# Two down projections of a macaron layer: block sums by accumulating transfers, operands and sums made at earlier steps, and a mixer planned from a running clock

## The chip, the cores and the metric

One Trainium2 chip, one of its cores. The metric is device time in microseconds of one launch, as the median over runs; the profile is one execution of the same program, read by the time from the first to the last of its own instructions (the span). All inputs and outputs are float32.

## The reference

One decoder layer on x of 512 tokens by 1024 channels; the middle mixer is only named here.

```python
D_MODEL, SEQ, D_FF = 1024, 512, 2816

def rmsnorm(x, g):
    return x * lax.rsqrt(jnp.mean(x * x, axis=-1, keepdims=True) + EPS) * g

def swiglu(x, w_gate, w_up, w_down):
    return (jax.nn.silu(x @ w_gate) * (x @ w_up)) @ w_down

x = x + 0.5 * swiglu(rmsnorm(x, ffn1_norm), ffn1_wg, ffn1_wu, ffn1_wd)
x = x + hybrid_mixer(rmsnorm(x, mix_norm), ...)   # sparse attention and a gated recurrence
x = x + 0.5 * swiglu(rmsnorm(x, ffn2_norm), ffn2_wg, ffn2_wu, ffn2_wd)
out = rmsnorm(x, final_norm)
```

## The kernel before, in words

**Precision.** TensorE multiplies in its rounded float32 form. To keep the precision of float32, each operand is split into a rounded part and a remainder: ScalarE (ACT) copies with rounding (`wh`, `yh`, the lower half of a `cm` tile), VectorE (DVE) subtracts that from the source (`wl`, `yl`, the upper half). A product is three matmuls: part by part, part by remainder, remainder by part. So whatever TensorE (PE) is to multiply passes ACT and then DVE first.

**Stages.** Up projection of the first feed-forward block, its down projection `d1`, the mixer, up projection and down projection `d2` of the second block, final norm. Both down projections are written by `block_down` (line 596); its steps are emitted one after the other, in the order in which every engine runs them (the schedule is manual; each engine runs its own instructions in the order of the program).

**A down projection.** D_FF is 22 tiles of 128 rows. Six tiles (`PLAIN`) are multiplied plainly, in steps `("D", half, k)`. The other sixteen form eight pairs (`PAIRS`), and for these a product of 2 by 2 blocks is made of seven products in place of eight (Strassen's scheme in Winograd's form), on sums and differences of blocks. Products are numbered 1, 2, 5, 6, 3, 7, 4 in the order in which they run, eight steps `(p, j)` each, one for each pair. So the steps are (line 604): six plain steps 0 to 5; products 1, 2 and 5 at 6 to 29; product 6 and then product 3, each of eight steps with two plain steps of the second half between them (30 to 39, 40 to 49); product 7 (50 to 57), two plain steps (58, 59), product 4 (60 to 67). In `d1` a step of a product is twelve matmuls of 256 columns, in `d2` six of 512; a plain step is twelve of 512.

**What a step needs.** Two things, both made some steps ahead by `task(i, f)`, which runs `f` behind step `i`:

- *A unit of weights*, split at step i - 4 (`unit`, `wsplit`). For products 1, 4 and 2 it is a block as loaded (`raws`, three buffers of 512 KB, loaded by SyncE's queue, SP). For the others it is a sum of blocks of the weights. Product 5's is block 2 + block 3: `base` loads block 2 with SP into `sums[j]`, `add` adds block 3 with an accumulating transfer that GpSimd (POOL) issues. Product 6's adds block 0 to it: `one` loads it with SP into a work tile (`a1`, four buffers), `second` adds it on DVE. Product 3's adds block 1 to that: `two` loads it with SP into another work tile (`a2`, three buffers), `fourth` adds it on DVE (lines 719 to 727). Product 7's is a sum of its own, block 2 + block 0, in a tile `s3[j]`: a load by SP at i - 15 and an add by POOL at i - 13.
- *An operand* made of the activations, split by `operand(p, j, soon)` `before` steps ahead (line 729): 9 for product 4, 5 for product 3. For product 4 the remainder is not made by DVE: ACT writes the negated rounded part, and POOL adds the source by an accumulating transfer within SBUF. Its source is written by a DVE subtraction one step earlier into the half `b(j)[:, hi]`, the half that product 3 reads.

`sums[j]` lies in two large tiles, four sums each, in `d1` (shown as `sm` in the profile) and in the tiles of x in `d2` (shown as `x`); `s3` tiles and operands (`cm`) are taken from a pool of 60 slots of 128 by 512 floats, which also holds the blocks of activations (`h`). DVE also adds each finished product to the residual (`x` in `d1`, `xr` in `d2`: `results1`, `results`), which must be done before PE may go on in the same bank: product 4 goes on in the banks that product 7 used.

**The end of `d1`.** While product 7 and product 4 run, the first four channel tiles of the mixer's operand are made (`norm_tile`, line 946, one each at steps 51, 53, 55 and 57), the others in two halves (`norm_round`), and their squares are summed into `acc`.

**The mixer.** Its 64 weight jobs run in an order written out by hand (`ORDER`, line 49): one job is one column tile of a projection. Everything else (norm, sparse attention, recurrence, gates) is a set of generators that `tick` (line 1183) advances between PE's matmuls as soon as a planner (`Plan`, line 60) says that their inputs will be there. The planner keeps a clock for each engine and a ready time for each tile, from fixed costs of each instruction. `plan.clear()` empties it behind `d1`, and `run_jobs` (line 1209) calls `plan.rewind()`, which sets all clocks to zero and forgets all ready times, and then gives `acc` a ready time of 2.6 us. The first five jobs (`i0 i1 k0 v0 e0`) use the unscaled operand `y`; the following ones use the normalised one, which exists once `acc` is complete, PE has summed and turned it, and eight tiles have been scaled and split.

All instructions are recorded under line 173 (the planner's `call`) and all transfers under line 161, so the profile is read by the tiles' names.

Of the kernel before, what the change touches and what calls it, by code (L numbers as in the profile page):

```python
# [12 lines left out]
ALU = mybir.AluOpType  # L13
# [33 lines left out]


ORDER = """
i0 i1 k0 v0 e0 q0 x0 x1 q1 x2 r1 x3 g0 q2 x4 g1 g2 q3 x5 g3 r2 x6  # L50
g4 r3 g5 x7 a0 r4 g6 a1 r5 g7 r6 a2 a3 a4 a5 r7 a6 a7 R0 R1 R2 R3
R4 R5 R6 A0 A1 A2 A3 A4 A5 A6 R7 A7 O0 O1 O2 O3 O4 O5 O6 O7
"""

V_G1, V_GM, V_G2, V_GF = 0, 8, 16, 24
# [4 lines left out]
class Plan:  # L60
# [8 lines left out]
    def clear(self):  # L69
        self.time = dict.fromkeys(("PE", "DVE", "ACT", "POOL", "SP", "DMA"), 0.0)  # L70
        self.ready, self.read, self.writer, self.table = {}, {}, {}, None
        self.live = {}

    def rewind(self):
        self.time = dict.fromkeys(self.time, 0.0)
        self.ready, self.read, self.writer = {}, {}, {}

    def seen(self, name, by):

# [99 lines left out]
def hybrid_kernel(ctx, tc, xt, vec, w1u, w1d, wm, wki, wrg, watt, wrnn, wout, w2u, w2d, gf, out):  # L179
    nc = tc.nc  # L180
    plan = Plan()
    V, A = plan.engine("DVE", nc.vector), plan.engine("ACT", nc.scalar)
    G, T = plan.engine("POOL", nc.gpsimd), plan.engine("PE", nc.tensor)
    Q = plan.engine("SP", nc.sync)
# [26 lines left out]
    def awork(name="a"):  # L211
        return patt.tile([P, S], F32, tag="att", name=nm(name))
# [383 lines left out]
    def block_down(hs, wd, sums):  # L596

        d = Down()
        steps = [("D", 0, k) for k in range(PLAIN)] + [(p, j) for p in (1, 2, 5) for j in range(PAIRS)]
        for p in (6, 3):
            for j in range(PAIRS):
                steps += [(p, j)] + [("D", 1, (6, 3).index(p) * 2 + j // 3)] * (j in (2, 5))
        steps += [(7, j) for j in range(PAIRS)] + [("D", 1, k) for k in (4, 5)] + [(4, j) for j in range(PAIRS)]
        index = {s: i for i, s in enumerate(steps)}
        tasks = {}  # L610

        def task(i, *fs):
            tasks.setdefault(i, []).extend(fs)

        def block(b, j):

            i, half = b * (PAIRS // 2) + j // 2, j % 2 * S
            return wd[i][:, half:half + S]

        units, turned, ra, raws, s3, ones, twos = {}, {}, {}, {}, {}, {}, {}  # L620

        def fetch(key, i):
            def load():
                raws[key] = raw.tile([P, WMAX], F32, tag="raw", name=nm("wr"))
                Q.dma_start(raws[key], wd[i])

            return load

        def unit(i, src):
            def split_():  # L630
                if i % 2 == 0:
                    units[i // 2] = [wsp.tile([P, WMAX], F32R, tag=t, name=nm(t)) for t in ("wh", "wl")]
                wsplit(src(), *(t[:, i % 2 * S:(i % 2 + 1) * S] for t in units[i // 2]))

            return split_

        a = lambda j: hs[PLAIN + 2 * j]
        b = lambda j: hs[PLAIN + 2 * j + 1]

        def differences(j):  # L640
            def subs():
                if j % 2 == 0:
                    ra[j // 2] = slot(F32, "cr")
                V.tensor_sub(ra[j // 2][:, (lo, hi)[j % 2]], a(j)[:, hi], b(j)[:, hi])
                V.tensor_sub(a(j)[:, hi], a(j)[:, hi], a(j)[:, lo])

            return subs

        SRC = {1: lambda j: a(j)[:, lo], 5: lambda j: a(j)[:, hi], 6: lambda j: a(j)[:, lo], 3: lambda j: b(j)[:, hi],
               7: lambda j: ra[j // 2][:, (lo, hi)[j % 2]], 4: lambda j: b(j)[:, hi], 2: lambda j: b(j)[:, lo]}  # L650

        def operand(p, j, soon):
            def make():
                o, src = slot(F32R, "cm"), SRC[p](j)
                turned[p, j] = o
                sign = -1.0 if p in (1, 3) else 1.0
                A.activation(o[:, lo], src, AF.Copy, scale=sign)
                if sign < 0:
                    V.scalar_tensor_tensor(o[:, hi], src, -1.0, f(o[:, lo]), op0=ALU.mult, op1=ALU.subtract)
                elif soon:  # L660
                    V.tensor_sub(o[:, hi], src, f(o[:, lo]))
                else:
                    A.activation(o[:, hi], src, AF.Copy, scale=-1.0)
                    G.dma_start(o[:, hi], src, accum_op=ALU.add)

            return make

        used = []
        for i, st in enumerate(steps):
            if st[0] == "D":  # L670
                _, h, k = st
                key = ("D", h, k // 2)
                if k % 2 == 0:
                    used.append([i - 4, index["D", h, k + 1] - 4, key, 2 * PAIRS + h * (PLAIN // 2) + k // 2])
                task(i - 4, unit(i, lambda key=key, k=k: raws[key][:, k % 2 * S:(k % 2 + 1) * S]))
                continue
            p, j = st
            if p in (1, 4, 2):
                key = (p, j // 2)
                if j % 2 == 0:  # L680
                    used.append([i - 4, index[p, j + 1] - 4, key, {1: 0, 2: 1, 4: 3}[p] * (PAIRS // 2) + j // 2])
                src = lambda key=key, j=j: raws[key][:, j % 2 * S:(j % 2 + 1) * S]
            elif p == 7:
                src = lambda j=j: s3[j]
            else:
                src = lambda j=j: sums[j]
            if p == 1:
                task(j, differences(j))
            if p == 5:
                def base(j=j):  # L690
                    Q.dma_start(sums[j], block(2, j))

                def add(j=j):
                    G.dma_start(sums[j], block(3, j), accum_op=ALU.add)

                task(j + 2, base)
                task(j + 4, add)
            if p == 7:
                def base(j=j):
                    s3[j] = slot(F32, "s3")  # L700
                    Q.dma_start(s3[j], block(2, j))

                def add(j=j):
                    G.dma_start(s3[j], block(0, j), accum_op=ALU.add)

                task(i - 15, base)
                task(i - 13, add)
            if p == 6:
                def one(j=j):
                    ones[j] = work("a1")  # L710
                    Q.dma_start(ones[j], block(0, j))

                def second(j=j):
                    V.tensor_add(sums[j], sums[j], ones[j])

                task(i - 9, one)
                task(i - 5, second)
            if p == 3:
                def two(j=j):
                    twos[j] = awork("a2")  # L720
                    Q.dma_start(twos[j], block(1, j))

                def fourth(j=j):
                    V.tensor_add(sums[j], sums[j], twos[j])

                task(i - 8, two)
                task(i - 5, fourth)
            soon = p != 4
            before = {1: 6, 6: 6, 7: i - j - 1, 4: 9}.get(p, 5)
            if p == 6:  # L730
                task(i - before - 1, lambda j=j: V.tensor_sub(a(j)[:, lo], b(j)[:, hi], a(j)[:, hi]))
            if p == 4:
                task(i - before - 1, lambda j=j: V.tensor_sub(b(j)[:, hi], b(j)[:, lo], a(j)[:, lo]))
            task(i - before, operand(p, j, soon))
            task(i - 4, unit(i, src))
        used.sort()
        for n, (first, last, key, i) in enumerate(used):
            at = first - 5
            if n >= RAWS:
                at = max(at, used[n - RAWS][1])  # L740
# [47 lines left out]
    y = []  # L788
# [14 lines left out]
    sums = []  # L803
# [139 lines left out]
    then1 = lambda i, f_, *a: late1.setdefault(i, []).append((f_, a))  # L943

    for k in range(KD // 2):
        then1(index[7, 0] + 1 + 2 * k, lambda k=k: y.append(norm_tile(k, V_GM)))
    rounds = {k: norm_round(k, hi) for k in range(KD // 2, KD)}
    for k in range(KD // 2, KD):
        then1(index[4, k - KD // 2], next, rounds[k], None)
# [4 lines left out]
    then1(index[4, 4], mixer_prepare)  # L954
    with tc.manual_schedule(engines=ENGINES):
        assert min(d1.tasks) >= 0
        cs = decay()
        for i in range(last):
            if i == 0:
# [42 lines left out]

    plan.clear()
    for h, l in y:
        plan.take("slot", h), plan.take("slot", l)
    follow = []
# [200 lines left out]
    def run_jobs():  # L1209
        ws = mixer_ws  # L1210
        mixer_fetch()
        mixer_fetch()
        plan.rewind()
        plan.ready[acc.name], plan.writer[acc.name] = 2.6, "DVE"
        for i, job in enumerate(jobs):
            ys, then = uses[job[0]](int(job[1:]))
            n, m = columns(job)
# [567 lines left out]
```

## Time and profile before

| what | us |
|---|---|
| median of 3 runs | 1084.09 |
| lowest and highest | 1083.97, 1086.08 |
| the profiled execution, in all | 1082.94 |
| its span | 1081.1 |
| PE, DVE, ACT, POOL busy | 1066.5, 863.3, 662.4, 139.9 |
| first down projection | 235 to 353 of the span |
| mixer | 353 to 730 |
| second down projection | 955 to 1074 |

How to read it. Times in the profile's rows are microseconds from the start of the span, unless they are marked ns. In a timeline a row is: start, duration, engine, line, operation, what it writes `<-` what it reads, shape, count, and in brackets the idle time of that engine before it and what ended it. A row of the chain is: start, length, engine and tile. A row of transfers is: tile `<-` source, issuing queue, operation, count, KB each, median us from issue to landing. A row of a window is: from:to, its length, then for PE, weight loads, DVE, ACT and POOL the busy time and the number of instructions, PE's granted clock, the mean busy share of the 16 DMA engines and GB/s. A matmul's recorded length is longer than the time until the next can start, so waits of PE are best read from start to start.

### The profile page before, as it was taken

To read this page: it belongs to the slowest core of one execution; us is meant where nothing else is said; L and a number is where in the kernel's file an instruction comes from. 1 tells how busy PE (TensorE), PEld (TensorE's weight loads), DVE (VectorE), ACT (ScalarE), POOL (GpSimd) and SP (SyncE) were. 2 spreads that over 40 slices of the span, in tenths; PEclk is the share of its full clock that TensorE was granted. 3 is DMA by queue.
4 is the path that set the end of the run, shared out by engine and by line. 5 is a ranking of instruction groups with operands and counts; after the bars stand their busy time and mean duration, and the time that the engine had idled before them with its cause. 6 is when DMAs were issued, how large, how long until landed. Compare 5 with 4: busy or idle time off the path is not lost.

```text
span 1081.1 us, 17665 instructions
## 1 busy us (share of the span) xinstructions
PE 1066.5 (99%) x6412; PEld 945.3 (87%) x6412; DVE 863.3 (80%) x1668; ACT 662.4 (61%) x1313; POOL 139.9 (13%) x171
## 2 busy tenths in 40 slices
PE   9999999999999999999999999999999999999997
PEld 7889999999988778888888888888899999987776
DVE  6687777779988879999799867666877777777887
ACT  6565655555547659868885664345656555565555
POOL 0161111102023000000000000002511111101022
PEclk9999999999999999999999999999999999999999
DMA  7297777739487452232232213435977777459395
GB/s 274 69 253 195 171 181 196 174 111 266 132 220 173 136 143 89 83 103 78 79 98 80 77 38 83 133 98 131 244 173 194 161 193 192 110 150 269 117 247 152
DMA packets 74007, 163.90 MB, mean 152 GB/s; under 512 B 8768, under 2 KB 17088, under 8 KB 73920
## 3 DMA queue, kind: packets, MB, share of 16 engines
q1 hardware_dynamic: 51216, 128.11, 36.6%
q0 software_dynamic: 22272, 34.09, 20.1%
q8 instruction: 50, 0.82, 0.3%
q10 hardware_dynamic: 432, 0.57, 0.1%
q14 instruction: 37, 0.30, 0.1%
HBM read 151.73 MB, written 2.10 MB: 142 GB/s over the span
## 4 chain that ended last, share of the span: by engine, by line
PE 85%; DVE 8%; ACT 2%; DMA 2%; issue 2%; SPq 0%; ACTq 0%; DVEq 0%
PE mm L173 59%; PE aux L173 27%; DVE wl L173 2%; ACT wh L173 1%; DMA wr<-w2d 1%; DVE x L173 1%; DVE sm L173 1%; DMA s<-w1d 1%; DVE yl L173 1%; DVE cm L173 1%; DMA x<-xt 0%; DVE acc L173 0%; DVE yf L173 0%; ACT yh L173 0%; DVE h L173 0%
## 5 line engine op out<-in xcount | busy, mean ns | idle before, releaser
L173 PE MATMUL mm<-cm,wh 128*128 128x256 f32 x1472 | 268.8, 283 | 1.6 <-DVE x L173 1.6
L173 DVE TENSOR_TENSOR wl<-wr,wh 128x512 fp32r<-128x512 f32 (+2 forms) x228 | 189.1, 833 | 78.1 <-ACT wh L173 77.8
L173 PEld LDWEIGHTS mm<-cm,wh 128*128 128x128 f32 x1472 | 229.9, 192 | 2.8 <-ACT cm L173 2.0
L173 PE MATMUL mm<-cm,wl 128*128 128x256 f32 x736 | 208.7, 284 | 0.7 <-DVE wl L173 0.7
L173 ACT ACTIVATE wh<-wr 128x512 fp32r<-128x512 f32 (+3 forms) x230 | 167.9, 736 | 51.7 <-issue 19.8
L173 PE MATMUL mm<-yh,wh 128*128 128x512 f32 (+1 forms) x416 | 164.2, 396 | 1.0 <-ACT yh L173 0.6
L173 PE MATMUL mm<-yl,wh 128*128 128x512 f32 (+1 forms) x416 | 162.5, 391 | 0.3 <-DVE yl L173 0.2
L173 PE MATMUL aux<-cm,wh 128*128 128x256 f32 x880 | 161.8, 283 | 0.0
L173 PE MATMUL mm<-yh,wl 128*128 128x512 f32 x408 | 159.3, 390 | 0.0
L173 PEld LDWEIGHTS mm<-cm,wl 128*128 128x128 f32 x736 | 141.2, 192 | 1.5 <-DVE wl L173 1.5
L173 PEld LDWEIGHTS aux<-cm,wh 128*128 128x128 f32 x880 | 137.3, 192 | 0.2 <-DMA cm<-cb 0.2
L173 DVE TENSOR_TENSOR wl<-s,wh 128x512 fp32r<-128x512 f32 x152 | 103.8, 687 | 27.1 <-ACT wh L173 25.3
L173 PE MATMUL aux<-cm,wl 128*128 128x256 f32 x440 | 124.5, 283 | 0.0
L173 ACT ACTIVATE wh<-s 128x512 fp32r<-128x512 f32 x152 | 92.4, 623 | 47.1 <-DVE s L173 30.9
L173 PEld LDWEIGHTS mm<-yh,wh 128*128 128x128 f32 (+1 forms) x416 | 78.0, 188 | 18.3 <-ACT yh L173 1.3
L173 PEld LDWEIGHTS mm<-yl,wh 128*128 128x128 f32 (+1 forms) x416 | 77.6, 187 | 16.5 <-DVE yl L173 1.6
L173 PEld LDWEIGHTS mm<-yh,wl 128*128 128x128 f32 x408 | 76.6, 188 | 16.5 <-DVE wl L173 0.2
L173 PEld LDWEIGHTS aux<-cm,wl 128*128 128x128 f32 x440 | 84.5, 192 | 0.0
L173 PE MATMUL mm<-wh,cm 128*128 128x512 f32 x192 | 59.9, 393 | 0.4
L173 ACT ACTIVATE tg<-mm 128x256 f32<-128x256 f32 x68 | 26.1, 384 | 52.8 <-PE mm L173 52.6
L161 POOL DMA_DIRECT2D cm<-cb x8 | 7.1, 883 | 336.1 <-DMA wr<-w2u 281.5
L161 POOL DMA_DIRECT2D s<-w2u x36 | 33.5, 1072 | 127.5 <-DMA s<-w2u 42.7
(244 smaller groups left out, 2021.6 us busy)
## 6 DMA issues: line engine op xcount, KB each, us to landing
wr<-wm SPq DMA_DIRECT2D x39, 512.0 KB, 3.5
wr<-w2u SPq DMA_DIRECT2D x26, 512.0 KB, 5.0
wr<-w1u SPq DMA_DIRECT2D x21, 512.0 KB, 5.3
wr<-w1d SPq DMA_DIRECT2D x18, 512.0 KB, 4.8
s<-w2u SPq DMA_DIRECT2D x36, 256.0 KB, 5.9
s<-w2u POOLq DMA_DIRECT2D x36, 256.0 KB, 5.4
wr<-w2d SPq DMA_DIRECT2D x18, 512.0 KB, 5.5
s<-w1u SPq DMA_DIRECT2D x32, 256.0 KB, 5.7
```

The costliest lines, as they stand in the source:

```text
L161: return self.engine.dma_start(out, src, **kw)
L173: return call(*args, **kw)
```

## The change

- Product 3's sums, in both down projections: `two` and the DVE addition go. `fourth` is now an accumulating transfer of block 1, issued by POOL, three steps before product 6 uses `sums[j]`, that is one step behind the emission of the split that reads it.
- Product 5's sums: load and add at steps 3j // 2 + 2 and + 4 instead of j + 2 and j + 4.
- Product 7's sums: load and add at i - 27 and i - 25 instead of i - 15 and i - 13, so steps 23 to 30 and 25 to 32.
- Product 4's operand: made at the step of product 3 with the same j (18 to 20 steps ahead instead of 9), from `a(j)[:, lo]` in place of `b(j)[:, hi]`.
- `d1`'s four norm tiles: at steps 51, 54, 57 and 59.
- Planner: cleared at the start of `d1`; behind `d1` only the held buffers are forgotten; `rewind` and the ready time given to `acc` are gone. A new `ORDER`, with the same 64 jobs.

```diff
 ORDER = """
-i0 i1 k0 v0 e0 q0 x0 x1 q1 x2 r1 x3 g0 q2 x4 g1 g2 q3 x5 g3 r2 x6
-g4 r3 g5 x7 a0 r4 g6 a1 r5 g7 r6 a2 a3 a4 a5 r7 a6 a7 R0 R1 R2 R3
-R4 R5 R6 A0 A1 A2 A3 A4 A5 A6 R7 A7 O0 O1 O2 O3 O4 O5 O6 O7
+i0 i1 k0 v0 e0 q0 q1 x0 x1 x2 r1 x3 g0 a0 x4 g1 g2 q2 q3 g3 r2 r3
+x5 a1 x6 r4 g4 x7 a2 g5 g6 r5 r6 g7 a3 a4 a5 r7 a6 a7 R0 R1 R2 R3
+R4 R5 R6 A0 A1 A2 A3 A4 A5 R7 A6 A7 O0 O1 O2 O3 O4 O5 O6 O7
 """
...
         SRC = {1: lambda j: a(j)[:, lo], 5: lambda j: a(j)[:, hi], 6: lambda j: a(j)[:, lo], 3: lambda j: b(j)[:, hi],
-               7: lambda j: ra[j // 2][:, (lo, hi)[j % 2]], 4: lambda j: b(j)[:, hi], 2: lambda j: b(j)[:, lo]}
+               7: lambda j: ra[j // 2][:, (lo, hi)[j % 2]], 4: lambda j: a(j)[:, lo], 2: lambda j: b(j)[:, lo]}
...
-                task(j + 2, base)
-                task(j + 4, add)
+                task(3 * j // 2 + 2, base)
+                task(3 * j // 2 + 4, add)
...
-                task(i - 15, base)
-                task(i - 13, add)
+                task(i - 27, base)
+                task(i - 25, add)
...
             if p == 3:
-                def two(j=j):
-                    twos[j] = awork("a2")
-                    Q.dma_start(twos[j], block(1, j))
-
                 def fourth(j=j):
-                    V.tensor_add(sums[j], sums[j], twos[j])
-
-                task(i - 8, two)
-                task(i - 5, fourth)
+                    G.dma_start(sums[j], block(1, j), accum_op=ALU.add)
+
+                task(index[6, j] - 3, fourth)
             soon = p != 4
-            before = {1: 6, 6: 6, 7: i - j - 1, 4: 9}.get(p, 5)
+            before = {1: 6, 6: 6, 7: i - j - 1, 4: i - index[3, j]}.get(p, 5)
...
             if p == 4:
-                task(i - before - 1, lambda j=j: V.tensor_sub(b(j)[:, hi], b(j)[:, lo], a(j)[:, lo]))
+                task(i - before - 1, lambda j=j: V.tensor_sub(a(j)[:, lo], b(j)[:, lo], a(j)[:, lo]))
...
-        then1(index[7, 0] + 1 + 2 * k, lambda k=k: y.append(norm_tile(k, V_GM)))
+        then1(index[7, 0] + (1, 4, 7, 9)[k], lambda k=k: y.append(norm_tile(k, V_GM)))
...
         assert min(d1.tasks) >= 0
+        plan.clear()
         cs = decay()
...
-    plan.clear()
+    plan.live = {}
...
-        plan.rewind()
-        plan.ready[acc.name], plan.writer[acc.name] = 2.6, "DVE"
```

More of the change, by code (lines that the diff above doesn't have):

```diff
@@ L72, in clear @@
         self.live = {}
-    def rewind(self):
-        self.time = dict.fromkeys(self.time, 0.0)
-        self.ready, self.read, self.writer = {}, {}, {}
     def seen(self, name, by):
@@ L618, in block @@
             return wd[i][:, half:half + S]
-        units, turned, ra, raws, s3, ones, twos = {}, {}, {}, {}, {}, {}, {}
+        units, turned, ra, raws, s3, ones = {}, {}, {}, {}, {}, {}
         def fetch(key, i):
```

## The prediction

> **What bounds the kernel now.** I read the page's busy times first, then who TensorE (PE) waited for, then the starts of PE's matmuls at the seams of the two down projections, then the chain and the other engines around each seam that came late.
>
> ```profile
> span 1081.1 us, 17665 instructions
> ...
> PE 1066.5 (99%) x6412; PEld 945.3 (87%) x6412; DVE 863.3 (80%) x1668; ACT 662.4 (61%) x1313; POOL 139.9 (13%) x171
> ```
>
> PE is the bound: 1066.5 of 1081.1 us. The change leaves its matmuls alone, so it can gain only PE's waits. The list of PE's waits shows which:
>
> ```profile
> PE mm L173 <- DVE x L173: 1.6, 1, 1.6
> ...
> PE aux L173 <- DVE acc L173: 1.0, 2, 0.8
> ...
> PE mm L173 <- ACT yh L173: 0.6, 1, 0.6
> ```
>
> The columns are the total, the number and the longest, in us. They undercount: a 256-wide matmul is recorded as 0.28 us long though the next can start 0.12 us later, so the first 0.16 us of a wait do not appear. So I measure phases from start to start, in PE's timeline. First down projection: the first matmuls of products 6, 3 and 7, of the two plain steps behind product 7, and of product 4.
>
> ```profile
> 286.23 0.40 PE L173 MATMUL mm<-cm,wh 128*128 128x256 f32 x2
> ...
> 303.23 0.40 PE L173 MATMUL mm<-cm,wh 128*128 128x256 f32 x2
> ...
> 322.20 0.40 PE L173 MATMUL mm<-cm,wh 128*128 128x256 f32 x2
> ...
> 333.72 0.40 PE L173 MATMUL aux<-hh,wh 128*128 128x512 f32 x1
> ...
> 340.95 0.36 PE L173 MATMUL mm<-cm,wh 128*128 128x256 f32 x1 [1.60 <-DVE x L173]
> ```
>
> Product 7 (eight steps) takes 11.52 us, 1.44 a step. Product 6 (eight steps and two plain ones) takes 17.00, so a plain step is (17.00 - 11.52) / 2 = 2.74. Product 3 has the same work as product 6 and takes 18.97: **1.97 us of waits**. The two plain steps take 7.23 where 5.48 would do: **1.75**. Second down projection: products 1, 2, 5, 6, 3 and 7.
>
> ```profile
> 974.50 0.39 PE L173 MATMUL mm<-wh,cm 128*128 128x512 f32 x1
> ...
> 985.38 0.39 PE L173 MATMUL aux<-wh,cm 128*128 128x512 f32 x1
> ...
> 998.73 0.39 PE L173 MATMUL mm<-wh,cm 128*128 128x512 f32 x1
> ...
> 1009.61 0.39 PE L173 MATMUL mm<-wh,cm 128*128 128x512 f32 x1
> ...
> 1028.01 0.50 PE L173 MATMUL mm<-wh,cm 128*128 128x512 f32 x1
> ...
> 1046.68 0.39 PE L173 MATMUL mm<-wh,cm 128*128 128x512 f32 x1
> ```
>
> Product 1 takes 10.88 (1.36 a step). Product 2 takes 13.35: **2.47** of waits. Products 6 and 3 should take 10.88 + 5.48 = 16.36 and take 18.40 and 18.67: **2.04** and **2.31**. With the mixer's start (1.0 + 0.6 us listed, three waits with 0.16 hidden each, about 2.1), all waits that the change can touch come to 12.6 us.
>
> **The change part by part.** *Product 3's sums.* The chain through product 3 of the first down projection is this loop:
>
> ```profile
> 303.63 0.61 DVE sm L173
> ...
> 304.27 0.64 ACT wh L173
> ...
> 304.93 0.34 DVE wl L173
> ...
> 305.54 0.69 DVE sm L173
> ```
>
> VectorE (DVE) adds the fourth block, ScalarE (ACT) rounds the sum, DVE makes the remainder: 305.54 - 303.63 = 1.91 us a step against PE's 1.44. The change takes eight adds of 0.61 us per projection from DVE, and with them the wait of DVE for ACT inside the loop. A step then costs DVE 0.60 (remainder) + 0.34 (operand) + 0.34 (the subtraction moved here from product 7's stretch) = 1.28, below 1.44 and 1.36. So 1.97 and 2.31 us go, if the sums arrive in time (below). Eight plain loads by SP go too; they cost nothing, since SP only queues.
>
> *Product 4's operands and product 7's sums.* Why was DVE late at 340.95?
>
> ```profile
> 321.31 8.40 DMA s<-w1d
> ...
> 340.05 0.76 DVE x L173 x2
> ```
>
> The chain runs from the last add of product 7's sums through DVE to there. In between DVE waits for ACT, which waits for such a sum, and does product 4's subtractions:
>
> ```profile
> 330.40 0.69 DVE L173 TENSOR_TENSOR wl<-s,wh 128x512 fp32r<-128x512 f32 x1 [0.98 <-ACT wh L173]
> 331.00 0.42 DVE L173 TENSOR_TENSOR h<-h,h 128x256 f32<-128x256 f32 x1
> ```
>
> The sums start 12 steps earlier, and eight subtractions (8 x 0.34 = 2.7 us) leave this stretch. Either is more than 1.75, so that wait goes. The norm tiles, now at steps 1, 4, 7 and 9 of the stretch instead of 1, 3, 5 and 7, are the same work in the same room. In product 3's stretch the moved operands bring ACT two copies, DVE one subtraction and GpSimd (POOL) one add a step; DVE and ACT have the room just counted. Tiles live longer: 16 blocks, 12 plain halves, 8 operands of product 7, 8 sums, some 7 operands in flight make 51 (53 with the gains) of 60 slots, so no wait there.
>
> *Product 5's sums, spread.* In the second projection product 2 waited for its weights:
>
> ```profile
> 982.24 9.86 DMA wr<-w2d
> ```
> ```profile
> 988.20 0.69 DVE L173 TENSOR_TENSOR wl<-wr,wh 128x512 fp32r<-128x512 f32 x1 [3.81 <-ACT wh L173]
> ...
> 992.87 0.69 DVE L173 TENSOR_TENSOR wl<-wr,wh 128x512 fp32r<-128x512 f32 x1 [1.50 <-ACT wh L173]
> ```
>
> What a transfer costs the 16 DMA engines I take from the queues (packets, MB, share of the span); q0 carries almost only POOL's adds:
>
> ```profile
> q1 hardware_dynamic: 51216, 128.11, 36.6%
> q0 software_dynamic: 22272, 34.09, 20.1%
> ```
>
> For 256 KB (0.262 MB): plain 0.366 x 1081.1 x 0.262 / 128.11 = 0.81 us, add 0.201 x 1081.1 x 0.262 / 34.09 = 1.67 us. Adds 4 and 5 now come behind these weights, which takes 3.3 us from in front of them; the later one was 1.5 us late. So the 2.47 go. DVE lost 3.81 + 1.50 us there and entered product 6 late; I count half of the 2.04 us, 1.1, as gained, since product 6's own loop, with its add on DVE, stays slower than PE.
>
> *What it costs: adds on POOL.* Each fourth block now waits on POOL until DVE has split the sum for product 6, and behind it wait product 7's adds, later fourth blocks and product 4's operands. First projection:
>
> ```profile
> 282.91 0.69 DVE L173 TENSOR_TENSOR wl<-sm,wh 128x512 fp32r<-128x512 f32 x1
> ```
>
> The first is free at 283.6. With the tasks' steps POOL's order is, from there (f a fourth block, s a sum of product 7): f0 s2 f1 s3 f2 s4 s5 f3 s6 f4 s7 f5 f6 f7. So f5 is twelfth, eleven intervals behind f0. Issuing takes POOL 0.86 us each, which it has (13% busy). PE wants it at product 3's sixth step, 303.23 + 5 x 1.44 + 2.74 = 313.2, so it must land by 312.4 to be rounded. How fast do adds land? Alone each is worth 1.67 us of the engines. Under load:
>
> ```profile
> 306.58 0.86 POOL L161 DMA_DIRECT2D s<-w1d  x1 [7.19 <-DVE cm L173]
> ```
> ```profile
> s<-w1d POOLq DMA_DIRECT2D x7, 256.0 KB, 7.7
> ```
>
> Seven adds, the first landing near 306.58 + 7.7 = 314.3, the last at 321.31 + 8.40 = 329.7: 2.57 us apart. The plain loads of that stretch (some 15 units of 256 KB, 12 us of engine time) keep the load up for about 14 us behind the first landing at 283.6 + 5.8 = 289.4 (5.8 is the middle of 7.7 and an unloaded 3.9). That is 5.6 intervals at 2.57 and 5.4 at 1.67: 312.8, or 0.4 late. Ends: 1.67 throughout gives 307.8, not late; 2.57 throughout gives 317.7, 5.3 late. I take 1.0 us for the first projection. In the second PE arrives 13 x 0.08 = 1 us sooner: 2.0 us (0 to 6.3). If the cover is gone, the wait is PE's whole.
>
> Can the denser transfers delay product 6's own block, which DVE needs in order?
>
> ```profile
> 282.16 0.33 SPq L161 DMA_DIRECT2D a<-w1d  x1
> ```
> ```profile
> 292.06 0.69 DVE L173 TENSOR_TENSOR sm<-sm,a 128x512 f32<-128x512 f32 x1
> ```
>
> Block 4 has 9.9 us; loads of 256 KB took less in the most loaded stretch (244 to 266 us), so nothing is charged:
>
> ```profile
> sm<-w1d SPq DMA_DIRECT2D x6, 256.0 KB, 6.4
> a<-w1d SPq DMA_DIRECT2D x4, 256.0 KB, 7.3
> ```
>
> *Mixer.* New order of jobs, and a plan whose clocks run on from the first down projection. Its start waits 2.1 us, behind a DVE that came late out of product 4; with DVE earlier I count 0.9 gained (the nearest row, 1.0 for acc, less a little). Ends: all 2.1 gained, or the same again lost, since an order cannot be read off the old trace. Later the mixer has nothing to gain:
>
> ```profile
> 500.00:550.00 50.00, 50.00 (x232) 41.33 (x231) 42.75 (x100) 41.52 (x73) 0.00 (x0) 1.00 0.27 85
> ```
>
> **Sum.** -1.97 - 1.75 + 1.0 in the first projection, -2.47 - 1.1 - 2.31 + 2.0 in the second, -0.9 in the mixer: **-7.5 us**. The profiled execution took 1082.94 us in all; 1075.4 from there. The median of the runs is 1084.09, 1.15 above it, so I forecast **1076.6**.
>
> **Rivals.** *The adds are never late* (nothing of the 3.0): -10.5, 1073.6. It needs landings at most (312.4 - 289.4) / 11 = 2.1 us apart; 1.67 speaks for it, 2.57 against. The Trainium skill, "DMA: Bandwidth & Descriptors", section "Anatomy of one DMA", puts a GpSimd transfer at 2.0 us + bytes / 436e3 per us; by that estimate another 256 KB takes 0.6 us and this rival holds. The trace disagrees with the page: an add costs 1.67 us of engine time.
>
> *One POOL queue, adds late: slower.* Place: product 3 in both projections. The gains without it are 10.5 us, so it decides once the two projections lose that much, some 5 us each: at landings about 2.57 us apart throughout, what the loaded row showed. Product 5's adds bound it worse: issued from 244.35 to 264.47 with a median of 7.0 us to land,
>
> ```profile
> 244.35 1.75 POOL L161 DMA_DIRECT2D sm<-w1d  x2 [33.41 <-DMA sm<-w1d]
> ...
> 264.47 0.86 POOL L161 DMA_DIRECT2D sm<-w1d  x1 [0.46 <-issue]
> ```
>
> 20.1 / 7 = 2.87 a landing, though some of that was waiting to be issued. At 2.87 f5 is at 289.4 + 31.6 = 321.0, 8.6 late, and 9.6 in the second: 18.2 - 10.5 = +7.7, **1091.8**. Against it: the plain loads run out.
>
> *The new order costs* 2.1 at or after the mixer's start instead of gaining 0.9: -4.5, 1079.6; were it twice that, 1081.7.
>
> **How the numbers follow.** Chances: forecast 0.45, adds never late 0.15, adds late 0.22, order costs 0.18. The first two are faster by over 0.2% (2.2 us, about what a measurement of this kernel can tell from no change); of the order's case two thirds are faster, the rest the same; of the late adds 0.16 are slower, the rest the same. Chances of an outcome that no row here warns of move some from faster to slower: faster 0.62, same 0.12, slower 0.26. The range reaches from a little below 1073.6 (a full gain at the mixer's start) to the middle of the late adds: 1072.0 to 1088.5. The forecast's own range is 1073 to 1080.
>
> **What would show it.** No DVE adds sm<-sm,a or x<-x,a but eight each; 16 POOL issues more onto sm and x. Product 3 near 18.0 us and 18.4, with PE or ACT waiting for a DMA onto sm or x near its sixth step: the price term. The wait for DVE x before product 4 gone. Product 2 of the second projection near 10.9. Wrong would be: PE waiting on an s or an a block, product 3 longer than 23 us, or PE idle inside the mixer for more than 3 us.

## The result, and the profile after

The changed kernel takes **1077.97 us** (median of 4 runs, 1076.80 to 1080.11), the kernel before 1084.97 beside it (4 runs, 1083.97 to 1086.08): a ratio of **0.9937, 95% interval 0.9917 to 0.9958**, 0.6% faster. The forecast was 1076.6, range 1072.0 to 1088.5. The profiled execution takes 1077.68 us (1082.94 before), 5.3 less, where the medians differ by 7.0.

The top of the page of the profile after, with the two large queues:

```profile
span 1075.9 us, 17646 instructions
...
PE 1063.4 (99%) x6412; PEld 945.3 (88%) x6412; DVE 852.6 (79%) x1652; ACT 662.0 (62%) x1313; POOL 154.6 (14%) x187
...
q1 hardware_dynamic: 48912, 123.92, 35.2%
q0 software_dynamic: 24576, 38.28, 22.1%
```

DVE has 16 instructions fewer and POOL 16 more: the adds moved as the diff says. PE has the same 6412 matmuls. Whom PE waited for (total us, times, longest):

```profile
PE mm L169 <- ACT wh L169: 2.3, 4, 0.7
...
PE mm L169 <- ACT yh L169: 0.6, 1, 0.6
...
PE aux L169 <- DVE acc L169: 0.2, 1, 0.2
```

The waits for DVE x (1.6) and most of that for acc (1.0) are gone. So are 1.4 us for ACT's rounded weights, wh, into aux (product 2 of the second projection). In their place stand 2.3 us for wh into mm, where it was 0.3. The matmuls at the seams of the first down projection, as before the first ones of products 6, 3 and 7, of the two plain steps and of product 4:

```profile
286.33 0.28 PE L169 MATMUL mm<-cm,wh 128*128 128x256 f32 x1
...
303.33 0.28 PE L169 MATMUL mm<-cm,wh 128*128 128x256 f32 x1
...
321.57 0.28 PE L169 MATMUL mm<-cm,wh 128*128 128x256 f32 x1
...
333.09 0.40 PE L169 MATMUL aux<-hh,wh 128*128 128x512 f32 x1
...
338.56 0.28 PE L169 MATMUL mm<-cm,wh 128*128 128x256 f32 x1
```

Product 3 takes 321.57 - 303.33 = 18.24 us (18.97 before, 17.00 without a wait), the two plain steps 5.47 (7.23 before). The second projection, first matmuls of products 1, 2, 5, 6, 3 and 7:

```profile
971.50 0.39 PE L169 MATMUL mm<-wh,cm 128*128 128x512 f32 x1
...
982.38 0.39 PE L169 MATMUL aux<-wh,cm 128*128 128x512 f32 x1
...
993.62 0.39 PE L169 MATMUL mm<-wh,cm 128*128 128x512 f32 x1
...
1004.50 0.39 PE L169 MATMUL mm<-wh,cm 128*128 128x512 f32 x1
...
1022.81 0.39 PE L169 MATMUL mm<-wh,cm 128*128 128x512 f32 x1
...
1041.52 0.39 PE L169 MATMUL mm<-wh,cm 128*128 128x512 f32 x1
```

Product 2 takes 11.24 (13.35 before), product 6 18.31 (18.40), product 3 18.71 (18.67). So the gain is in product 2 and ahead of product 4; product 3 of the second projection got nothing. Where PE stopped in product 3, with ACT's rows for the sum that it stopped for (the bracket is the idle time and what ended it):

```profile
310.53 0.63 ACT L169 ACTIVATE wh<-sm 128x512 fp32r<-128x512 f32 x1 [1.09 <-DMA sm<-w1d]
...
313.24 0.63 ACT L169 ACTIVATE wh<-sm 128x512 fp32r<-128x512 f32 x1 [1.16 <-DMA sm<-w1d]
```
```profile
313.92 0.39 PE L169 MATMUL mm<-cm,wh 128*128 128x256 f32 x1 [0.49 <-ACT wh L169]
...
1031.71 0.50 PE L169 MATMUL mm<-wh,cm 128*128 128x512 f32 x1 [0.58 <-ACT wh L169]
...
1034.33 0.50 PE L169 MATMUL mm<-wh,cm 128*128 128x512 f32 x1 [0.67 <-ACT wh L169]
```

PE waits for ACT, and ACT for the transfer that adds the fourth block to the sum: the sixth one, as forecast, at 313.24. When are the adds issued? POOL's rows in that stretch (the second number is the time of the issue, or of several in a row):

```profile
284.66 0.88 POOL L157 DMA_DIRECT2D sm<-w1d  x1 [5.41 <-DVE cm L169]
...
291.22 1.75 POOL L157 DMA_DIRECT2D s<-w1d  x2 [2.10 <-DMA s<-w1d]
...
296.24 0.86 POOL L157 DMA_DIRECT2D s<-w1d  x1 [2.37 <-DMA s<-w1d]
296.77 1.22 POOL L157 DMA_DIRECT2D sm<-w1d  x1
300.43 0.86 POOL L157 DMA_DIRECT2D s<-w1d  x1 [2.44 <-DMA s<-w1d]
300.96 3.00 POOL L157 DMA_DIRECT2D sm<-w1d  x3
```

sm is a fourth block, s a sum of product 7. Three times POOL stands still (2.10, 2.37, 2.44 us) before an add of product 7, because the plain load that this add goes onto has not landed; the first fourth block is issued at 284.66, the fifth at 296.77, and the last three, behind the third of these waits, together at 300.96. The transfers of 283 to 309 us, median time to landing last:

```profile
sm<-w1d POOLq DMA_DIRECT2D x8, 256.0 KB, 12.5
...
s<-w1d SPq DMA_DIRECT2D x5, 256.0 KB, 5.9
```

A plain load takes 5.9 us, and its add is only two steps (2.9 us) behind it. An issued fourth block takes 12.5 us. The first and the sixth by themselves:

```profile
sm<-w1d POOLq DMA_DIRECT2D x1, 256.0 KB, 6.2
...
sm<-w1d POOLq DMA_DIRECT2D x1, 256.0 KB, 12.2
```

The first lands at 284.66 + 6.2 = 290.9, the sixth at 300.96 + 12.2 = 313.2, eleven adds later: 2.0 us an add. From issue and time to landing, all the adds between them land in the order of their issue, 1.2 to 3.3 us apart, and six of them are issued but have not landed when the sixth fourth block is issued. So there were adds under way all the time that POOL stood still. What makes the sixth late is the number of adds ahead of it times their spacing; that POOL's standing still adds to it is not shown here, and e9 speaks against it.

### The profile page after: what moved, and what is told of

Read it like the earlier page. It is cut to its first block, busy times and chain, and to the rows that moved or that the text cites. A ratio compares the mean times of both kernels' runs of the same rounds, so it can differ in the third digit from the quotient of the medians.

```text
span 1075.9 us, 17646 instructions
## 1 busy us (share of the span) xinstructions
PE 1063.4 (99%) x6412; PEld 945.3 (88%) x6412; DVE 852.6 (79%) x1652; ACT 662.0 (62%) x1313; POOL 154.6 (14%) x187
## 4 chain that ended last, share of the span: by engine, by line
PE 83%; DVE 7%; DMA 5%; ACT 2%; issue 1%; SPq 0%; POOL 0%; ACTq 0%; POOLq 0%; DVEq 0%
PE mm L169 59%; PE aux L169 25%; DVE wl L169 2%; ACT wh L169 1%; DMA sm<-w1d 1%; DMA x<-w2d 1%; DMA a<-w2d 1%; DMA s<-w1d 1%; DMA wr<-w2d 1%; DVE cm L169 1%; DVE yl L169 1%; DVE ca L169 1%; ACT cm L169 1%; DVE h L169 0%; DVE yf L169 0%
```

## The experiments

For all kernels I cut both projections at PE's plain steps (matmuls with an hh or hl operand) and took each stretch start to start. The table gives by how much each stretch is longer than the shortest of its kind in any of these profiles, in us. "Product 3" runs from the plain step in product 6's sixth to the one behind product 7; "product 2" from product 1's start to the first plain step in product 6; "mixer" from product 4's start to the second projection's (shortest 613.37). The first two columns of numbers are the median time and the ratio to before with its 95% interval; before's own median beside them was 1084.5 to 1084.9. The other columns are of one profiled execution each, which lies up to 2.5 us above the median (e1 2.1, e4 2.5, e9 2.3) or below it (e10 1.2).

| kernel | us | ratio | 1st: prod. 6 | 1st: prod. 3 | 1st: ahead of 4 | 2nd: prod. 2 | 2nd: prod. 6 | 2nd: prod. 3 | mixer |
|---|---|---|---|---|---|---|---|---|---|
| before | 1084.97 | 1 | 0.0 | 1.97 | 1.76 | 2.65 | 1.61 | 2.56 | 0.97 |
| after | 1077.97 | 0.9937 (0.9917-0.9958) | 0.0 | 1.23 | 0.0 | 0.64 | 1.59 | 2.43 | 0.36 |
| e1 | 1076.66 | 0.9930 (0.9912-0.9948) | 1.49 | 0.0 | 0.0 | 3.34 | 1.61 | 0.03 | 0.26 |
| e2 | 1079.00 | 0.9948 (0.9932-0.9963) | 0.0 | 0.0 | 0.0 | 2.28 | 1.61 | 0.01 | 3.94 |
| e3 | 1081.99 | 0.9973 (0.9964-0.9983) | 0.96 | 1.72 | 0.0 | 2.05 | 1.62 | 3.20 | 0.38 |
| e4 | 1083.27 | 0.9986 (0.9977-0.9996) | 1.38 | 1.73 | 0.0 | 0.71 | 1.61 | 2.96 | 5.55 |
| e5 | 1078.64 | 0.9939 (0.9926-0.9952) | 0.0 | 2.05 | 0.0 | 1.32 | 1.61 | 3.01 | 0.0 |
| e6 | **1072.97** | 0.9885 (0.9868-0.9903) | 0.0 | 0.0 | 0.0 | 0.0 | 1.62 | 0.03 | 0.02 |
| e7 | **1072.30** | 0.9878 (0.9863-0.9893) | 0.0 | 0.0 | 0.0 | 0.20 | 0.0 | 0.0 | 0.04 |
| e8 | 1076.96 | 0.9922 (0.9910-0.9935) | 0.59 | 0.0 | 0.0 | 2.76 | 1.60 | 0.01 | 0.07 |
| e9 | 1076.21 | 0.9918 (0.9905-0.9931) | 0.61 | 0.41 | 0.0 | 1.73 | 1.63 | 2.85 | 0.02 |
| e10 | 1077.31 | 0.9931 (0.9918-0.9943) | 0.0 | 0.0 | 0.0 | 0.48 | 1.60 | 0.01 | 2.31 |

My theory behind the prediction: product 3 is freed of DVE's adds, and what it then waits for are the adding transfers, late because product 7's early ones stand between them on POOL's one queue. Rivals: the moved copies of product 4's operands make ACT late; product 7's and product 4's moves are what ends the wait before product 4; the mixer's order is worth something of its own.

**e1: the kernel before, with the fourth block's add alone.**

```
             if p == 3:
                 def fourth(j=j):
-                    V.tensor_add(sums[j], sums[j], twos[j])
-                task(i - 8, two)
-                task(i - 5, fourth)
+                    G.dma_start(sums[j], block(1, j), accum_op=ALU.add)
+                task(index[6, j] - 3, fourth)
```

> The kernel before, with the fourth block of product 3's sums added by a POOL transfer and nothing else of the change. Queue theory (product 3 waits for adds that stand behind others in the one POOL queue, and DVE's relief is the gain): product 7's adds now come behind the fourth blocks, so no fourth block is late: product 3 near 17.0 us in the first projection and 16.4 in the second (before 18.97 and 18.67). SP is no longer held up by the work tiles of the fourth blocks, so product 7's sums come sooner by themselves; the wait before product 4 (1.75) falls to 0.5 or less. Product 2 of the second projection keeps its 2.47, product 6 its 2.04. In all 5 to 6 us below the kernel before. Rival 1 (product 7's sums and product 4's operands must be moved to free product 4): 1.75 stays, 4.2 below. Rival 2 (the late steps of product 3 after the change come from ACT, which got product 4's copies): the same here as the queue theory, since nothing is moved.

Measured 1076.66 us, 8.0 below the kernel before where 5 to 6 were expected: this one edit gives all of the change's gain. Product 3 has no wait in either projection, and the wait ahead of product 4 is gone too, though product 7's sums and product 4's operands are where they were in the program. Two things have changed for DVE ahead of product 4. It has lost the eight adds; and product 7's sums land sooner without being moved, as expected: the last one 2.6 us behind product 7's first matmul, where it was 7.5, so that ACT, which waited 3.2 us for these sums before, no longer waits for them. DVE's last addition to x ends only 0.2 us before product 4 starts. Which of the two ended the wait, e1 cannot tell. What stays are waits for product 2's weights, the longest of them here:

```profile
990.71 0.50 PE L173 MATMUL aux<-wh,cm 128*128 128x512 f32 x1 [1.94 <-ACT wh L173]
```

In the first projection these weights came late as well; PE did not feel it there, but DVE lost 1.44 us ahead of product 6, which fits the 1.49 us more that product 6 took:

```profile
269.00 0.69 DVE L173 TENSOR_TENSOR wl<-wr,wh 128x512 fp32r<-128x512 f32 x1 [1.44 <-ACT wh L173]
```

**e2: the changed kernel, with product 7's sums back at their old place.**

```
-                task(i - 27, base)
-                task(i - 25, add)
+                task(i - 15, base)
+                task(i - 13, add)
```

> The changed kernel with product 7's sums back at i - 15 and i - 13. Queue theory: the fourth blocks no longer stand behind product 7's adds, so product 3 falls from 18.24 and 18.71 us to 17.0 to 17.2 and 16.4 to 16.8; product 7's sums still come in time, since SP is not held up, and the wait before product 4 stays gone (5.5 for the two plain steps). 3 to 3.6 us below the changed kernel. Rival 1 (product 7's sums are late again): product 3 falls likewise, but up to 1.75 come back before product 4; 1.5 to 2 below. Rival 2 (ACT's copies for product 4 make product 3 late): product 3 stays at 18.2 and 18.7, no gain.

Measured 1079.00, 1.0 above the changed kernel, where 3 to 3.6 below it were expected. Product 3 is free of waits in both projections (1.23 and 2.43 in the changed kernel), so the early sums are what delays the fourth blocks. Yet the whole is no faster: product 2's weights came late again (2.28), and the attention behind the first projection, where neither the kernel before nor the changed one stops, now does, and the mixer's stretch is 3.94 us long over the shortest:

```profile
651.22 0.50 PE L169 MATMUL aux<-ptl,VV 128*128 128x512 f32 x1 [0.90 <-DVE ptl L169]
...
654.33 0.50 PE L169 MATMUL mm<-ath,wh 128*128 128x512 f32 x1 [1.20 <-ACT ath L169]
```

**e3: the changed kernel, with product 5's sums at one a step again.**

```
-                task(3 * j // 2 + 2, base)
-                task(3 * j // 2 + 4, add)
+                task(j + 2, base)
+                task(j + 4, add)
```

> The changed kernel with product 5's loads and adds back at steps j + 2 and j + 4. Theory (the adds in front of product 2's weights delayed them): product 2 of the second projection goes from 11.24 us back to about 13.3, the rest stays: 2 us above the changed kernel. Rival (the weights came late because their buffers were free late, and came sooner for another reason): product 2 stays near 11.2, no difference.

Measured 1081.99, 4.0 us above the changed kernel, twice what was expected. Product 2 of the second projection waits again, 2.05 us in all; that is 1.4 us of it. The rest is where nothing was expected: product 6 of the first projection takes 0.96 us more, and product 3 waits 0.5 and 0.8 us longer.

```profile
991.42 0.50 PE L169 MATMUL aux<-wh,cm 128*128 128x512 f32 x1 [1.31 <-ACT wh L169]
```

**e4: the changed kernel, with product 4's operands nine steps ahead, as before.**

```
-               7: ..., 4: lambda j: a(j)[:, lo], 2: ...
+               7: ..., 4: lambda j: b(j)[:, hi], 2: ...
-            before = {..., 4: i - index[3, j]}.get(p, 5)
+            before = {..., 4: 9}.get(p, 5)
-                task(..., V.tensor_sub(a(j)[:, lo], b(j)[:, lo], a(j)[:, lo]))
+                task(..., V.tensor_sub(b(j)[:, hi], b(j)[:, lo], a(j)[:, lo]))
```

> The changed kernel with product 4's operands made 9 steps ahead again, in product 7's stretch. Queue theory: product 3 stays at 18.2 and 18.7 us, since its adds stand as they did; in the first projection DVE has 2.7 us more in product 7's stretch, but no late sums to wait for, so the wait before product 4 is 0 to 0.8. In all 0 to 0.8 us above the changed kernel. Rival 2 (ACT's copies for product 4 make product 3 late): product 3 falls to 17.0 to 17.4 and 16.4 to 17.0, 2 to 3.5 us below.

Measured 1083.27, 5.3 above the changed kernel, where 0 to 0.8 were expected. Without the moved copies on ACT product 3 waits as long as with them (1.73 and 2.96 us), still for a transfer through ACT; the rival about ACT falls. The wait ahead of product 4 does not come back, and product 6 waits 1.38 us in the first projection. The mixer's stretch is the longest of all, 5.55 us over the shortest.

```profile
316.24 0.50 PE L169 MATMUL mm<-cm,wh 128*128 128x256 f32 x2 [0.54 <-ACT wh L169]
```

The attention stops at the same places as in e2, for as long (0.90 and 1.20 us), though here product 7's sums are early. Behind these stops PE's granted clock (the last column but two) falls in this execution, which no other profile shows there:

```profile
660.00:665.00 5.00, 4.97 (x15) 3.94 (x16) 2.94 (x5) 1.26 (x3) 0.00 (x0) 0.66 0.20 52
```

A clock of 0.66 over 5 us loses 1.7 us, about what e4's stretch has over e2's (1.6). So some 3.9 us go with the stops, and the rest with the clock of this execution, the slowest of ten.

**e5: the changed kernel, with the mixer as it was,** the old list ORDER among it.

```
         assert min(d1.tasks) >= 0
-        plan.clear()
...
-    plan.live = {}
+    plan.clear()
...
         mixer_fetch()
+        plan.rewind()
+        plan.ready[acc.name], plan.writer[acc.name] = 2.6, "DVE"
```

> The changed kernel with the mixer as it was: the old order of jobs, and the planner's clocks rewound at the mixer. Theory (the new order and the running plan gain nothing of their own, the 0.6 us less from product 4 to the second projection come from VectorE being earlier): that stretch stays at 613.6 to 613.8 us, and the whole time within 0.5 us of the changed kernel, 1077.5 to 1078.5. Rival (the order took the wait out of the mixer's start): the stretch is back at 614.3 to 614.7, the time 0.6 to 0.9 us above the changed kernel.

Measured 1078.64; the intervals of the two overlap. The stretch from product 4's first matmul to the second projection's first, in e5 and in the changed kernel (whose first end, 338.56, is shown above):

```profile
339.62 0.28 PE L173 MATMUL mm<-cm,wh 128*128 128x256 f32 x1
...
952.99 0.47 PE L173 MATMUL aux<-wh,hh 128*128 128x512 f32 x1
```
```profile
952.29 0.47 PE L169 MATMUL aux<-wh,hh 128*128 128x512 f32 x1
```

613.37 us with the old mixer, 613.73 with the new: the whole gain at the mixer's start is there without the new order and the running plan, which together take 0.36 of it back (0.38 in e3).

**e6: product 7's sums late and the mixer as it was** (the edits of e2 and e5 together; that is the fourth block's add, product 4's early operands, product 5's spread and the norm tiles).

> The changed kernel with product 7's sums at their old, late place and the mixer as it was. Theory (product 7's early sums delay the fourth blocks on the one queue, and the running plan carries a bad order into the attention when they move): product 3 takes the clean 17.0 and 16.3 us, the stretch from product 4 to the second projection 613.6 to 613.8 instead of 617.3, no wait before product 4: 3 us below the changed kernel less up to 1.6 us of varying waits for product 2's weights, 1074.5 to 1076.5. Rival (the attention stalls because the late sums leave VectorE late for the mixer, whatever the plan): the stretch stays near 617, the time near 1079.

Measured **1072.97 us, 5.0 below the changed kernel**, lower than the theory gave, since product 2's weights came in time as well. Product 3 and the mixer's stretch are clean. POOL's rows beside those of the changed kernel show why:

```profile
294.35 0.86 POOL L161 DMA_DIRECT2D sm<-w1d  x1 [1.12 <-DVE wl L173]
...
301.75 0.86 POOL L161 DMA_DIRECT2D sm<-w1d  x1 [1.13 <-DVE wl L173]
302.29 3.90 POOL L161 DMA_DIRECT2D s<-w1d  x4
```
```profile
sm<-w1d POOLq DMA_DIRECT2D x8, 256.0 KB, 7.8
```

Each fourth block leaves as soon as DVE has split its sum (the bracket names DVE's wl, no transfer), the last at 301.75, and only then product 7's adds; a fourth block lands after 7.8 us instead of 12.5, with no add of product 7 in front of it.

**e7: as e6, and product 6's block added by a transfer too.**

```
-                def one(j=j):
-                    ones[j] = work("a1")
-                    Q.dma_start(ones[j], block(0, j))
                 def second(j=j):
-                    V.tensor_add(sums[j], sums[j], ones[j])
-                task(i - 9, one)
-                task(i - 5, second)
+                    G.dma_start(sums[j], block(0, j), accum_op=ALU.add)
+                task(index[5, j] - 3, second)
```

> As the run with late sums and the old mixer, and product 6's block also added by a transfer, issued once product 5's operand is split, in place of a load and a VectorE add. Theory (product 6 of the second projection is held by its own loop over VectorE and ScalarE, 1.9 us a step against 1.36): product 6 there falls from 18.3 to about 16.5 us, the time 1.5 to 2 us below the run before, 1073 to 1074.5. Rival (the loop was not it, VectorE enters late for want of product 2's weights, and eight more adds of 1.67 us of engine time in place of loads of 0.81 only put these weights and the sums further behind): product 6 stays at 18.3 or longer, product 2 waits 2 us or more, the time 1 to 5 us above the run before.

Measured 1072.30, a little below what the theory gave. The stretch with product 6's fourth to sixth steps in the second projection, in the changed kernel and in e7 (start of its plain step to the next plain step):

```profile
1008.93 0.40 PE L169 MATMUL aux<-wh,hh 128*128 128x512 f32 x1
...
1017.32 0.39 PE L169 MATMUL aux<-wh,hh 128*128 128x512 f32 x1
```
```profile
1007.31 0.39 PE L173 MATMUL aux<-wh,hh 128*128 128x512 f32 x1
...
1014.11 0.39 PE L173 MATMUL aux<-wh,hh 128*128 128x512 f32 x1
```

8.39 us against 6.80. All the other kernels have 1.6 us more there, however late DVE entered. It goes with DVE's add, so it is product 6's own loop over DVE and ACT. From the second projection's start to its product 4 e7 takes 101.08 us, e6 102.53. The medians differ by 0.67 only, and their intervals overlap: that e7 is the faster is shown for this stretch, not for the whole.

**e8: as e6, with product 5's sums at one a step again** (the edit of e3 on e6).

> As the run with late sums and the old mixer, with product 5's sums at one a step again. Theory (spreading them takes adds from in front of product 2's weights): product 2 of the second projection waits 2 to 3 us more in a stall for these weights near its fifth step, and the first projection's product 6 comes 1 to 1.5 us later after the same stall of VectorE; the time 1.5 to 3 us above the run before, 1076.5 to 1078.5. Rival (the waits for product 2's weights differ from run to run by as much, whatever the spread): the time within 0.7 us of the run before.

Measured 1076.96, 4.0 above e6, with intervals apart. The second projection's product 2 stretch is 2.76 us longer; PE's wait there, and ACT's for the weights:

```profile
989.46 0.73 PE L173 MATMUL aux<-wh,cm 128*128 128x512 f32 x2 [2.01 <-ACT wh L173]
```
```profile
988.77 0.63 ACT L173 ACTIVATE wh<-wr 128x512 fp32r<-128x512 f32 x1 [5.71 <-DMA wr<-w2d]
```

Over all profiles the four kernels with dense sums (before, e1, e3, e8) have 2.05 to 3.34 us there, the eight with spread sums 0 to 2.28: the spread helps, by 1.8 us between the means, but the wait is near its edge and comes back in some. e8 also answers another question: it differs from e1 by product 4's early operands and the moved norm tiles alone, and takes as long (1076.96 and 1076.66, ratios 0.9922 and 0.9930). So these two moves are worth nothing that can be measured, and what e6 has over e1 is the spread of product 5's sums.

**e9: as e5, with product 7's adds five steps behind their plain loads.**

```
                 task(i - 27, base)
-                task(i - 25, add)
+                task(i - 22, add)
```

> The changed kernel with the mixer as it was, and product 7's adds five steps behind their plain loads instead of two (loads at 27, adds at 22 steps ahead). Theory (GpSimd stands in front of product 7's adds until their plain loads have landed, three waits of 2.1 to 2.4 us, and the fourth blocks behind it are late for that): these waits go, the fourth blocks move ahead of three more adds, and product 3 falls from 18.9 and 18.7 to 17.0 to 17.6 and 16.3 to 17.2 us; the time 1.5 to 4 us below the run with early sums and the old mixer, 1074.5 to 1077. Rival (adds land no faster than they did, about two microseconds apart, whatever GpSimd waits for): the sixth fourth block still lands near 313 us, product 3 within 0.5 us of before, the time 1078 to 1079.

Measured 1076.21, 2.4 below e5 (their intervals overlap a little). POOL no longer stands in front of product 7's adds for their loads:

```profile
293.07 0.86 POOL L161 DMA_DIRECT2D sm<-w1d  x1 [1.82 <-DVE wl L173]
293.61 1.22 POOL L161 DMA_DIRECT2D s<-w1d  x1
...
297.14 0.86 POOL L161 DMA_DIRECT2D sm<-w1d  x1 [0.32 <-DMA sm<-w1d]
```
```profile
sm<-w1d POOLq DMA_DIRECT2D x1, 256.0 KB, 15.0
```

Product 3 of the first projection falls from 2.05 to 0.41 us of wait; that of the second only from 3.01 to 2.85. The time is what the theory gave, but not for its reason. The sixth fourth block (the last row) is now issued 6 us earlier than in e5 and takes 15.0 us to land instead of 11.1: it lands at 312.1, 2.1 us earlier. Of that 0.6 us is the first fourth block's earlier landing; from there on it is ten adds of 2.3 us, against eleven of 2.2 in e5. The adds land no faster, as the rival had it; the later adds of product 7 have let this block go ahead of one more of them. In the second projection the sixth block also gains one place, but the last one falls from the fourteenth place to the sixteenth, and PE waits for it (0.40 us at 1040.59) as well as for the sixth (0.68 at 1034.19). So the price of the early sums is the places that they take on the queue, in both projections; POOL's standing still is not needed to explain it.

**e10: as e6, with the new list ORDER, the planner's clocks rewound at the mixer as before** (e6 with ORDER as in the change's diff).

> The run with late sums and the old mixer, with the new order of jobs in the mixer but the planner's clocks rewound there as before. Theory (the running clocks carry the earlier work's order into the attention's plan): the stretch from product 4 to the second projection stays at 613.4 to 613.8 us, the time within 0.6 us of the run with the old order, 1072.5 to 1073.5. Rival (the new order of jobs itself costs when the sums are late): the stretch is near 617, the time near 1077.

Measured 1077.31, the time of the rival; the mixer's stretch of 615.68 lies between the two expectations (its execution took 1076.14). Of the 3.94 us that e2 loses there, 2.31 thus come with the new order of jobs alone and the other 1.6 with the running clocks on top of it; the running clocks with the old order were not run. PE's longest stop is again the attention's:

```profile
654.46 0.50 PE L173 MATMUL mm<-atl,wh 128*128 128x512 f32 x1 [1.58 <-DVE atl L173]
```

**e11: e2 once more,** one run of 1078.05 us.

> The changed kernel with product 7's sums late, a second profile of the same kernel. If the 2.3 us that its second projection's product 2 lost against the run with the old mixer belong to the kernel, products 1, 2 and 5 take 39.1 us again and the attention stalls again at 651 to 656 us; if they come from one execution to the next, 36.7 to 37.5.

The attention's stops came back to the hundredth (0.90 and 1.20 us), and the mixer's stretch within 0.05 us (617.36). Products 1, 2 and 5, with product 6's first three steps, took 37.81 us against 39.07 in e2 and 36.79 in e6. So 1.3 of the 2.3 us differ between two executions of one kernel: single differences of about a microsecond in the columns of product 2 say nothing.

## Why the prediction was right, and where its steps failed

The sum was -7.5 us; the profiled execution lost 5.3. The time lies in the range, 1.4 us above the forecast, and product 3 waits at the sixth fourth block as foreseen. The terms:

- **DVE's adds out of product 3** (-1.97 and -2.31, before the price): right, and shown by e1 and e2, where product 3 has no wait left.
- **The price, late adds on the one queue** (+1.0 and +2.0): right in place and in mechanism, near in size, 1.23 and 2.43 by the table. The order of the fourteen adds on the queue is the forecast one, and the sixth fourth block lands eleven adds behind the first. The two numbers of the sum were each off, and nearly cancelled, which is luck: the first landed at 290.9 and not 289.4, and the eleven intervals took 22.3 us and not 23.4 (seven of 2.4 us, then four of 1.3, where the forecast had 5.6 of 2.57 and 5.4 of 1.67). That POOL "has room" for its issues overlooked that it stands still in front of product 7's adds until their plain loads land, 6.9 us in all; by the landings and e9 that is not what the price comes from. *The adds are never late* fell by a little: it needed at most 2.1 us an add with the first at 289.4; there were 2.03, but the first was later. The Trainium skill, "DMA: Bandwidth & Descriptors", section "Anatomy of one DMA", would by estimate give 0.6 us an add; the trace has 1.2 us at the least.
- **The wait ahead of product 4** (-1.75, measured -1.76): right in size; of the reasons, one step was not needed and one is open. I named the moved sums of product 7 and product 4's subtractions; e1 has moved neither, and the wait is gone. There DVE has eight adds less, and product 7's sums land 4.9 us sooner against product 7 by themselves; which of the two does it is not shown. In e2 and e11 ACT waits for these sums again (1.8 and 3.1 us), and PE does not, with product 4's operands made early. In any case the move that cost 1.2 and 2.4 us was not needed, and the price was avoidable.
- **Product 5's spread** (-2.47): 2.0 in the profile and 1.8 between the means; right, a little large for product 2. The times of e3 and e8 say 4.0 for the whole, since the late sums and weights cost time in other places too.
- **Product 6 of the second projection** (-1.1): failed. I ascribed half of its 2.04 us to DVE's late entry. The 1.6 us in its middle stayed in every kernel but e7, so they were its own loop; the product as a whole went from 18.40 to 18.31.
- **The slower rival** (adds 2.57 to 2.87 us apart throughout, 1091.8) did not come: the eleven intervals were 2.03 us on average, since the last four were short.
- **Mixer** (-0.9): the term for DVE coming earlier was right (e5: 0.97). The new order and the running plan, which I bounded but gave no value, cost 0.36 here, and 2.3 to 3.9 where the first projection's changes are others (e10, e2; in e4 some 3.9 too, without the loss of clock).

The missing 2.2 us are thus product 6 (1.1), product 5's spread (0.5), the late adds (0.7) and the mixer (0.3), less some 0.3 by which the second projection's product 3 had more to gain (2.56 by the table, 2.31 in the sum). The median came only 1.4 us above the forecast, because the profiled execution stands 0.3 below its median now and stood 1.15 below it before.

What stays open: which of the planner's choices makes the attention stop when product 7's sums or product 4's operands are late (e2, e4), since I compared the outcomes and not the planned orders; which of two things ended the wait ahead of product 4; and what moves the landing of product 2's weights by a microsecond from one execution to the next.

## What to carry to other kernels

A change of several parts should be priced part by part: here one edit alone gave 8 us (e1), the spread of product 5's sums 4 more (e3, e8), and of the two moves that were not needed one took 3.7 us of this back, by standing in front of the first edit's adds on a single queue. On a queue in order count what stands ahead of the entry that is needed first, and how far apart entries land; in e9 an issue 6 us earlier gained little more than the one place that came with it. A list or a plan that is tuned to one timing is to be tuned again, or left alone, when the work ahead of it moves.

## What the runs showed of the hardware that I had not expected

The busy time of the DMA engines by packets is no exclusive time. In product 6 of the second projection of the changed kernel the mean share (the last column but one) is above one:

```profile
1008.93:1017.32 8.39, 8.19 (x31) 5.24 (x30) 7.58 (x16) 3.50 (x8) 3.62 (x5) 1.00 1.10 272
```

1.10 of 16 engines means that the times of packets overlap; over the 25 us from 290 to 315 it is 1.10 as well. A price worked out as share by span by bytes (my 1.67 us an add) is therefore no lower bound, and 1.36 us an add was seen.
